# Three taps of a depthwise convolution moved from VectorE to TensorE, and small first-stage operations to ScalarE

## The chip, the core and the metric

The kernel runs on one core of a Trainium2 chip. The metric is device microseconds of one execution on that core. TensorE, VectorE, ScalarE and GpSimd are called by their names or, as the profile has them, PE, DVE, ACT and POOL; SP (SyncE) issues nearly all DMAs. PEld is TensorE's weight load, which overlaps its products.

## What is computed

A trunk of one layer on 1024 frames of width 1024, all float32: a combined input projection feeds a convolution group and an RWKV-7 group side by side, then follow a joint output projection, cross-attention into 256 memory tokens and a squared-ReLU MLP. The part that the change touches is the convolution group's depthwise convolution, and next to it the token shift of the RWKV group:

```python
def conv_group(pa, conv_w, conv_b, ln_g, ln_b):
    u = pa[..., :CONV_WIDTH] * jax.nn.sigmoid(pa[..., CONV_WIDTH:])
    u = lax.conv_general_dilated(          # 31 taps, causal, 512 channels
        u, conv_w[:, None, :].astype(u.dtype), window_strides=(1,),
        padding=[(CONV_K - 1, 0)], dimension_numbers=('NWC', 'WIO', 'NWC'),
        feature_group_count=CONV_WIDTH) + conv_b
    ...                                    # layer norm over channels, silu

def rwkv7_group(pb, mu_b, ...):
    prev = jnp.pad(pb, ((0, 0), (1, 0), (0, 0)))[:, :-1]
    z = (pb + mu_b * (prev - pb)).astype(jnp.float32)
    ...                                    # r, k, v, three LoRA gates, the recurrence
```

## The kernel before

Channels lie on the 128 partitions and frames along the free axis. The 512 convolution channels are four blocks `c`; the frames are two halves `h` of 512.

**First stage (`mixer_in`, line 521).** Eight row blocks of `x` are normalised and transposed into `hT`. For each `c` and `h`, `conv` (line 540) runs two projections of 24 products each (`project`, three fp32r products for each of eight 128-row pieces): the gate, to which ScalarE applies a sigmoid into a tile `sg`, and the value, which VectorE multiplies into `sg` (line 545). A DMA writes `sg` to the DRAM array `du`. Between the (c, h) steps stand five products of the LoRA gates (`lora_out`, line 660). The tiles `sg`, the LoRA results and the later `z` share one ring of four buffers (`ZB`). Then come the r, k, v projections of the first half (`pair_steps(..., 0)`, twelve projections) and, in the second half, twelve more beside the start of the recurrence. Each of them ends in `shift_mix` (line 505): ScalarE scales the projection into `z`, VectorE adds the shifted part (line 511), then ScalarE copies the last column into `prev` (line 515, first half) or VectorE corrects column 0 from it (line 517, second half). The weights of the next projections pass `weight` (line 259): ScalarE rounds `wst` to `whi` (line 266), GpSimd subtracts for `wlo` (line 267), and TensorE needs both.

**The taps (`tap_steps`, line 609).** VectorE runs the convolution in five blocks: two of 512 frames for c = 0 and three of 1024 for c = 1 to 3. Of each block it loads `u` from `du`, makes the first tap with the bias (line 624), adds 30 taps one by one into `acc` (line 627), and a DMA stores `acc` to the DRAM array `dc` (line 632). There is one buffer of `u` and one of `acc`. `conv_norms` reads `dc` later.

**What sets the order.** A scheduler orders each engine's instructions ahead of time by priority; an engine then runs its list strictly in that order. `tap` (line 605) hands out the next taps at a priority 1000 steps ahead of the work around them, so that they fill VectorE early. PSUM banks are handed out in a fixed ring of eight while this stage lasts (`bank`, line 65). Other lines touched: `mixer_constants` (line 166, four scaled masks on VectorE) and `memory_in` (line 433, two scalings of 1024 columns on VectorE).

**After it.** The recurrence (`front`, `chain`) runs over eight blocks of 128 frames, with side work between its steps, until about 600 us; then output projection, attention and the MLP.

Of the kernel before, what the change touches and what calls it, by code (L numbers as in the profile page):

```python
# [9 lines left out]
F32 = mybir.dt.float32  # L10
# [17 lines left out]
GROUPS = PAIRS // GROUP  # L28
ORDER = ((1, 5, 6, 7, 4, 2, 3), (1, 6, 7, 5, 4, 2, 3))
TAPS = 31  # L30
HEADS = 8
N = 64
C = 64
# [18 lines left out]
class Trunk:  # L52
# [100 lines left out]
    def mixer_constants(self, pb, tmp):  # L153
        nc, a = self.nc, self.a

        bones = tmp.tile([P, P], F32, name="bones")
        nc.vector.memset(bones, 0.0)
        nc.vector.memset(bones[0:64, 0:64], 1.0)
        nc.vector.memset(bones[64:128, 64:128], 1.0)
        self.cent = pb.tile([P, P], F32, name="cent")  # L160
        nc.vector.scalar_tensor_tensor(self.cent, bones, -1.0 / N, self.ident, ALU.mult, ALU.add)
        self.bones_r = pb.tile([P, 4, P], F32, name="bones_r")
        self.bones_k = pb.tile([P, 4, HEADS], F32, name="bones_k")
        nc.vector.memset(self.bones_k, 0.0)
        for p in range(4):
            nc.vector.tensor_scalar(self.bones_r[:, p, :], bones, self.col("r_k", p), None, ALU.mult)
            kk = self.col("k_k", p)
            nc.vector.tensor_scalar(
                self.bones_k[:, p, 2 * p : 2 * p + 2], bones[:, 0:128:64], kk, kk, ALU.mult, ALU.mult
            )  # L170

        self.spread = pb.tile([HEADS, 4, P], F32, name="spread")
        nc.sync.dma_start(
            self.spread, a["k_k"][0:1, :].rearrange("o (p f) -> o p f", f=P).broadcast_to([HEADS, 4, P])
        )

        nc.gpsimd.affine_select(
            self.spread, self.spread, pattern=[[P, 4], [1, P]], compare_op=ALU.is_ge, fill=0.0,
            base=0, channel_multiplier=-N,
        )  # L180
        nc.gpsimd.affine_select(
            self.spread, self.spread, pattern=[[-P, 4], [-1, P]], compare_op=ALU.is_ge, fill=0.0,
            base=N - 1, channel_multiplier=N,
        )

        self.mask = pb.tile([P, P], F32, name="mask")
        nc.gpsimd.memset(self.mask, 1.0)
        for lo in (0, 64):
            m = self.mask[lo : lo + 64]
            nc.gpsimd.affine_select(  # L190
                m[:, 0:64], m[:, 0:64], pattern=[[1, 64]], compare_op=ALU.is_gt, fill=0.0,
                base=0, channel_multiplier=-1,
            )
            nc.gpsimd.affine_select(
                m[:, 64:128], m[:, 64:128], pattern=[[1, 64]], compare_op=ALU.is_ge, fill=0.0,
                base=0, channel_multiplier=-1,
            )

        self.reset = pb.tile([P, 8, C], F32, name="reset")
        nc.gpsimd.memset(self.reset, 1.0)  # L200
        nc.gpsimd.memset(self.reset[:, :, 0:1], 0.0)
# [223 lines left out]
    def memory_in(self, px):  # L425
# [3 lines left out]
        for i in range(2):  # L429
            t = px.tile([P, D], F32, tag="x", name="mem", bufs=4)  # L430
            nc.sync.dma_start(t, self.a["mem"][0, i * P : (i + 1) * P, :])
            _, r = self.rms_scale(px, t)
            nc.vector.tensor_scalar(t, t, r, None, ALU.mult)
            ts.append(t)
        for k in range(KC):
            pp = self.bank(self.ps, "mm")
# [68 lines left out]
    def shift_mix(self, dst, pp, j, h, m):  # L505
# [8 lines left out]
        if h == 0:  # L514
            nc.scalar.copy(self.prev[:m, j : j + 1], pp[:, HALF - 1 : HALF])
        else:
            nc.vector.scalar_tensor_tensor(
                dst[:, 0:1], self.prev[:m, j : j + 1], mu, dst[:, 0:1], ALU.mult, ALU.add
            )

    def mixer_in(self, pc, pb, px, pl, pW, pz, hT):
        nc, a = self.nc, self.a
# [17 lines left out]
        def conv(c, h, wg, wv):  # L540
# [3 lines left out]
            pv = self.project(wv, hT, h, P)  # L544
            nc.vector.tensor_tensor(sg, pv, sg, ALU.mult)
            nc.sync.dma_start(self.du[c, :, h * HALF : (h + 1) * HALF], sg)
            self.conved.add((c, h))

        def conv_weights(c):
# [8 lines left out]
                t = norm(i + 1)  # L558
        self.constants(pc, px)
        ts = [norm(4), norm(5)]  # L560
        conv(0, 0, *w)
        self.tap(TE[0], TE[3])
        self.mixer_constants(pb, px)
        features(ts.pop(0), 4)
# [8 lines left out]
        features(ts.pop(0), 6)  # L573
        features(ts.pop(0), 7)
        zl[0] += (self.lora_gate(pl, lora, hT, 0),)
        conv(0, 1, *w)
        zl.append(self.lora_in(pl, lora, hT, 1) + (self.lora_gate(pl, lora, hT, 1),))
        lora = itertools.chain.from_iterable(self.lora_out(pz, h, *zl[h]) for h in range(2))
        for c in range(1, 4):
            w = conv_weights(c)  # L580
            for h in range(2 if c < NC else 1):
                conv(c, h, *w)
                for _ in range(LO):
                    next(lora, None)
                self.tap(2 * TAPA)
            if c == 3:
                self.memory_in(px)
        self.conv, self.conv_weights = conv, conv_weights
        for _ in self.pair_steps(pW, pz, hT, 0):
            next(lora, None)  # L590
            self.tap(TAPA)
# [3 lines left out]
    def second_half(self, pW, pz, hT):  # L595
        pairs = self.pair_steps(pW, pz, hT, 1)
        for c in range(NC, 4):
            self.conv(c, 1, *self.conv_weights(c))
            yield
            for _ in range(12 // (4 - NC)):  # L600
                next(pairs)
# [7 lines left out]
    def tap_steps(self, pV):  # L609

        nc = self.nc
        for c in range(4):
            for h in range(2) if c < HC else (None,):
# [7 lines left out]
                else:  # L621
                    nc.sync.dma_start(u, self.du[c, :, t0 - TAPS + 1 : t0 + n])
                acc = pV.tile([P, S], F32, tag="acc", name="acc")[:, 0:n]
                nc.vector.tensor_scalar(acc, u[:, 0:n], self.cw[:, c : c + 1], self.col("conv_b", c), ALU.mult, ALU.add)
                yield
                for t in range(1, TAPS):
                    nc.vector.scalar_tensor_tensor(  # L627
                        acc, u[:, t : t + n], self.cw[:, t * 4 + c : t * 4 + c + 1], acc, ALU.mult, ALU.add
                    )
                    if t < TAPS - 1:  # L630
                        yield
                nc.sync.dma_start(self.dc[c, :, t0 : t0 + n], acc)
                yield
# [940 lines left out]
```

## Time and profile before

| | |
|---|---|
| median of 3 runs | 1570.99 us (1570.08 to 1573.53) |
| the profiled execution | 1570.75 us |
| its span, first to last instruction | 1569.0 us |
| mean granted TensorE clock | 0.978 of 2.4 GHz |
| TensorE busy | 1496.6 us, 95% of the span |
| VectorE busy | 1168.3 us, 74% |
| ScalarE busy | 665.6 us, 42% |
| GpSimd busy | 533.1 us, 34% |

The shares are averages over stages that differ. A stage is read by a window: busy time of each engine in a stretch, and the clock that TensorE was granted in it (1.00 is 2.4 GHz, 0.50 is 1.2 GHz). What an engine lacks to the length of the stretch is idle time. A timeline row that ends in brackets gives the idle time just before it and what ended it; its first number is the start and the second the length of the row, for all its instructions together (their ends overlap, since an engine is pipelined).

### The profile page before, as it was taken

What the parts mean: (1) busy time and instruction counts of PE and PEld (TensorE: products, weight loads), DVE (VectorE), ACT (ScalarE), POOL (GpSimd) and SP (SyncE); (2) the same over time, 40 slices, a digit from 0 to 9 for tenths busy, and PEclk for the clock granted to TensorE, in tenths of its full rate; (3) what the DMA queues carried; (4) which work ended last, traced back from release to release, by engine and by line L of the source; (5) the groups of instructions that cost most, each with busy time, mean ns of one, the idle gap of its engine ahead of it and who ended that gap; (6) DMA issues with size and microseconds to landing.
All of it is one profiled execution on the core that took longest, in us unless ns stands there. A gap on an engine that the chain in (4) does not pass through costs nothing. (4 is left out here: it accounts for less than half of the span.)

```text
span 1569.0 us, 22055 instructions
## 1 busy us (share of the span) xinstructions
PE 1496.6 (95%) x8114; PEld 1220.9 (78%) x8114; DVE 1168.3 (74%) x1721; ACT 665.6 (42%) x1223; POOL 533.1 (34%) x435
## 2 busy tenths in 40 slices
PE   5998888899999999999999979999999899999998
PEld 4677666778877778888888858888888788888886
DVE  5989898997889988475443787766566487587995
ACT  4423223122556553344230355555555445444454
POOL 4212237432444532431110064545444330003362
PEclk9999998897999999999999989999999999999999
DMA  7144336346334532312110132444444495562323
GB/s 236 47 134 162 115 114 175 113 124 183 108 100 129 151 108 88 101 47 81 41 41 28 48 126 96 163 153 160 148 158 158 155 377 190 185 194 87 102 80 122
DMA packets 175725, 201.14 MB, mean 128 GB/s; under 512 B 12191, under 2 KB 116951, under 8 KB 175618
## 3 DMA queue, kind: packets, MB, share of 16 engines
q1 hardware_dynamic: 168706, 187.15, 38.1%
q10 hardware_dynamic: 6912, 12.59, 2.2%
q8 instruction: 64, 1.05, 0.3%
q14 instruction: 43, 0.35, 0.1%
HBM read 139.92 MB, written 59.77 MB: 127 GB/s over the span
## 5 line engine op out<-in xcount | busy, mean ns | idle before, releaser
L627 DVE SCALAR_TENSOR_TENSOR acc<-u,cw,acc 128x1024 f32<-128x1024 f32 (+1 forms) x150 | 205.0, 1367 | 3.8
L267 POOL TENSOR_TENSOR wlo<-wst,whi 128x1024 fp32r<-128x1024 f32 (+2 forms) x34 | 86.9, 2557 | 133.0 <-ACT whi L266 133.0
L1236 POOL TENSOR_TENSOR p<-p,p 128x512 f32<-128x512 f32 x32 | 60.9, 1932 | 197.8 <-DVE p L1495 174.1
L73 DVE TENSOR_TENSOR s<-f,s 128x512 fp32r<-128x512 f32 x48 | 51.1, 1068 | 53.3 <-ACT s L72 53.3
L1341 ACT ACTIVATE y<-y 128x512 f32<-128x512 f32 x64 | 40.4, 632 | 81.0 <-DVE y L1236 73.3
L73 DVE TENSOR_TENSOR s<-y,s 128x512 fp32r<-128x512 f32 x57 | 44.9, 790 | 22.8 <-ACT s L72 22.8
L95 POOL TENSOR_TENSOR rsr<-rsv,mhalf 128x1 f32<-128x1 f32 x26 | 15.2, 585 | 137.1 <-DVE rsv L90 133.5
L455 PE MATMUL mm<-memT,wkv 128*128 128x256 f32 x256 | 61.7, 387 | 0.0
L1236 POOL TENSOR_TENSOR s<-y 128x512 f32<-128x512 f32 x32 | 41.1, 1306 | 59.8 <-ACT y L1342 56.5
L72 ACT CAST s<-y 128x512 fp32r<-128x512 f32 x57 | 35.2, 621 | 58.2 <-PE us L83 26.8
L266 ACT CAST whi<-wst 128x1024 fp32r<-128x1024 f32 (+2 forms) x34 | 35.0, 1030 | 57.6 <-PE pr L82 12.3
L891 DVE TENSOR_TENSOR fs<-xt,PL 128x4 f32<-128x4 f32 (+15 forms) x128 | 54.8, 428 | 5.8 <-ACT PL L883 3.0
L72 ACT CAST r<-y 128x512 fp32r<-128x512 f32 x55 | 33.8, 620 | 55.7 <-PE cp L83 23.2
L81 PE MATMUL mm<-hT1hi,whi 128*128 128x512 f32 (+1 forms) x120 | 51.1, 426 | 5.2 <-DVE z L511 3.0
L73 DVE TENSOR_TENSOR r<-y,r 128x512 fp32r<-128x512 f32 x55 | 42.8, 782 | 13.7 <-ACT r L72 13.7
L83 PE MATMUL mm<-hT1hi,wlo 128*128 128x512 f32 (+1 forms) x120 | 49.9, 416 | 2.6 <-POOL wlo L267 2.6
L72 ACT CAST s<-w 128x512 fp32r<-128x512 f32 x69 | 42.6, 619 | 21.8 <-DMA w<-in_w_ff_dram 6.9
L455 PEld LDWEIGHTS mm<-memT,wkv 128*128 128x128 f32 x256 | 46.7, 191 | 6.2
L1079 POOL TENSOR_TENSOR wql<-wst,wqh 128x1024 fp32r<-128x1024 f32 x8 | 20.0, 2498 | 88.3 <-ACT wqh L1078 88.3
L82 PE MATMUL mm<-hT1lo,whi 128*128 128x512 f32 (+1 forms) x120 | 49.7, 414 | 0.0
L72 ACT CAST s<-f 128x512 fp32r<-128x512 f32 x64 | 38.0, 620 | 27.4 <-DVE f L1236 21.9
L892 DVE TENSOR_REDUCE xt<-fs 128x2 f32<-128x4 f32 (+15 forms) x128 | 45.2, 353 | 3.1
(1142 smaller groups left out, 4961.7 us busy)
## 6 DMA issues: line engine op xcount, KB each, us to landing
y<-da SPq DMA_DIRECT2D x112, 256.0 KB
wst<-in_w_in_dram SPq DMA_DIRECT2D x32, 512.0 KB
w<-in_w_ff_dram SPq DMA_DIRECT2D x56, 256.0 KB
da<-y ACTq DMA_DIRECT2D x48, 256.0 KB
ms<-in_w_ff_dram SPq DMA_DIRECT2D x16, 512.0 KB
w<-in_w_ff_dram SPq DMA_DIRECT2D x16, 512.0 KB
da<-s SPq DMA_DIRECT2D x32, 256.0 KB
da<-y SPq DMA_DIRECT2D x32, 256.0 KB
```

The lines of the kernel that those rows point to most:

```text
L72: nc.scalar.copy(hi, src)
L73: (eng or nc.vector).tensor_tensor(lo, src, f32(hi), ALU.subtract)
L81: nc.tensor.matmul(ps, lh, rh, start=first and k == 0, stop=False)
L82: nc.tensor.matmul(ps, lh, rl, start=False, stop=False)
L83: nc.tensor.matmul(ps, ll, rh, start=False, stop=last and k == n - 1)
L267: nc.gpsimd.tensor_tensor(lo, st, f32(hi), ALU.subtract)
L455: nc.tensor.matmul(dst, w[:, k, :], mem[k // 4][:, k % 4, :], start=k == 0, stop=k == KC - 1)
L627: nc.vector.scalar_tensor_tensor(acc, u[:, t : t + n], self.cw[:, t * 4 + c : t * 4 + c + 1], acc, ALU.mult, ALU.add)
L891: nc.vector.tensor_tensor(tmp, x, rows, ALU.mult)
L892: nc.vector.tensor_reduce(xt[:, 0:m, 2 * k : 2 * k + 2], tmp, AX.X, ALU.add)
L1236: (eng or self.nc.vector).tensor_tensor(out, x, y, op)
L1341: nc.scalar.activation(c, c, AF.Relu)
```

## The change

With `PETAPS = 3`, the last three taps (offsets 0, 1 and 2 back from the current frame) no longer run on VectorE. A new function `late_taps` builds for each `c` three diagonal 128x128 matrices of the tap weights on ScalarE, multiplies them on TensorE with `sg` shifted by 0, 1 and 2 columns into one PSUM bank (float32 operands), and adds for the second half two narrow products with the last two columns of the first half (`edge`). ScalarE adds the bias into a tile `part` from the ring of four, and a DMA writes it to `dc`. `tap_steps` then loads `acc` from `dc` instead of making the first tap, and adds 28 taps. A block counts as ready (`conved`) after `late_taps`. Besides, the four scaled masks, the two memory scalings and the correction of column 0 in `shift_mix` go from VectorE to ScalarE.

```diff
-            nc.vector.tensor_scalar(self.bones_r[:, p, :], bones, self.col("r_k", p), None, ALU.mult)
+            nc.scalar.activation(self.bones_r[:, p, :], bones, AF.Identity, scale=self.col("r_k", p))
...
-            nc.vector.tensor_scalar(t, t, r, None, ALU.mult)
+            nc.scalar.activation(t, t, AF.Identity, scale=r)
...
         else:
-            nc.vector.scalar_tensor_tensor(
-                dst[:, 0:1], self.prev[:m, j : j + 1], mu, dst[:, 0:1], ALU.mult, ALU.add
-            )
+            nc.scalar.activation(dst[:, 0:1], self.prev[:m, j : j + 1], AF.Identity, bias=dst[:, 0:1], scale=mu)
...
+        def late_taps(c, h, sg):
+
+            if h == 0:
+                self.edge = pl.tile([P, PETAPS - 1], F32, tag="edge", name="edge")
+                nc.scalar.copy(self.edge, sg[:, HALF - PETAPS + 1 :])
+                self.diag = []
+                for j in range(PETAPS):
+                    t = pl.tile([P, P], F32, tag=f"dg{j}", name="diag")
+                    k = (TAPS - 1 - j) * 4 + c
+                    nc.scalar.activation(t, self.ident, AF.Identity, scale=self.cw[:, k : k + 1])
+                    self.diag.append(t)
+            pp = self.bank(self.ps, "mm")
+            for j in range(PETAPS):
+                nc.tensor.matmul(
+                    pp[:, j:], self.diag[j], sg[:, : HALF - j], start=j == 0, stop=h == 0 and j == PETAPS - 1
+                )
+            for j in range(1, PETAPS) if h else ():
+                nc.tensor.matmul(
+                    pp[:, :j], self.diag[j], self.edge[:, PETAPS - 1 - j :], start=False, stop=j == PETAPS - 1
+                )
+            z = pz.tile([P, HALF], F32, tag="z", name="part", bufs=ZB)
+            nc.scalar.activation(z, pp, AF.Identity, bias=self.col("conv_b", c))
+            nc.sync.dma_start(self.dc[c, :, h * HALF : (h + 1) * HALF], z)
             self.conved.add((c, h))
...
-                conv(c, h, *w)
-                for _ in range(LO):
+                made = conv(c, h, *w)
+                for k in range(LO):
+                    if k == 2:
+                        late_taps(*made)
                     next(lora, None)
...
-                nc.vector.tensor_scalar(acc, u[:, 0:n], self.cw[:, c : c + 1], self.col("conv_b", c), ALU.mult, ALU.add)
-                yield
-                for t in range(1, TAPS):
+                nc.sync.dma_start(acc, self.dc[c, :, t0 : t0 + n])
+                for t in range(TAPS - PETAPS):
                     nc.vector.scalar_tensor_tensor(
                         acc, u[:, t : t + n], self.cw[:, t * 4 + c : t * 4 + c + 1], acc, ALU.mult, ALU.add
                     )
```

The scheduler orders the new program anew; from the attention on, the lists of all engines read as before.

On TensorE, before the change, the products of step (1, 1) follow the five LoRA products after step (1, 0) without a break (`hT1` is the second half of the frames, `zw` and `za` feed the LoRA products):

```order
L666 MATMUL cp<-zw,l_w_decay 128x512
L666 MATMUL mm<-zw,l_w_decay 128x512
L666 MATMUL pr<-zw,l_w_decay 128x512
L666 MATMUL py<-zw,l_w_decay 128x512
L666 MATMUL us<-za,l_a_lora 128x512
L81 MATMUL mm<-hT1hi,whi 128x512
```

With the change the three products with the diagonals of step (1, 0) stand eighteen products into the gate projection of step (1, 1), and the first of them waits for VectorE, which makes `sg`:

```order
L83 MATMUL cp<-hT1lo,whi 128x512
L84 MATMUL cp<-hT1hi,wlo 128x512
L561 MATMUL us<-sg,diag 128x512 [waits DVE_49]
L561 MATMUL us<-sg,diag 128x511
L561 MATMUL us<-sg,diag 128x510
L82 MATMUL cp<-hT1hi,whi 128x512
```

All products behind it in TensorE's list wait with it; there are eight such places.

On VectorE, where the last convolution step (3, 1) ends and the first r, k, v projections follow, before the change (`acc<-u,cw,acc` is a tap, `sg` the product of value and gate, `z` the shift of a projection):

```order
L627 SCALAR_TENSOR_TENSOR acc<-u,cw,acc 128x1024 x8
L545 TENSOR_TENSOR sg<-mm,sg 128x512
L627 SCALAR_TENSOR_TENSOR acc<-u,cw,acc 128x1024 x5
L511 SCALAR_TENSOR_TENSOR z<-pr,pcol,z 128x511
L624 TENSOR_SCALAR acc<-u,cw,pcol 128x1024
L627 SCALAR_TENSOR_TENSOR acc<-u,cw,acc 128x1024
L511 SCALAR_TENSOR_TENSOR z<-py,pcol,z 128x511
```

With the change:

```order
L652 SCALAR_TENSOR_TENSOR acc<-u,cw,acc 128x1024 x6
L544 TENSOR_TENSOR sg<-cp,sg 128x512
L652 SCALAR_TENSOR_TENSOR acc<-u,cw,acc 128x1024 x8
L512 SCALAR_TENSOR_TENSOR z<-pr,pcol,z 128x511
L652 SCALAR_TENSOR_TENSOR acc<-u,cw,acc 128x1024 x4
L512 SCALAR_TENSOR_TENSOR z<-py,pcol,z 128x511
```

Before, the block c = 1 ends with the five taps ahead of the first `z`; now it ends with the six ahead of `sg`, and the next block's first eight taps, with the wait for its loads, stand ahead of the first `z`.

On VectorE, in the first block of the recurrence, beside the r, k, v projections of the second half, before the change (`kk`, `AR`, `a`, `BK`, `kp`, `T` belong to the recurrence):

```order
L813 TENSOR_TENSOR kk<-pr,zk 128x512
L627 SCALAR_TENSOR_TENSOR acc<-u,cw,acc 128x1024
L511 SCALAR_TENSOR_TENSOR z<-mm,pcol,z 128x511
L517 SCALAR_TENSOR_TENSOR z<-prev,pcol,z 128x1
L834 SCALAR_TENSOR_TENSOR AR<-kk,W 128x8x64
L835 TENSOR_TENSOR a<-a,kk 128x512
L627 SCALAR_TENSOR_TENSOR acc<-u,cw,acc 128x1024
L836 TENSOR_TENSOR BK<-a,sig 128x8x64
L627 SCALAR_TENSOR_TENSOR acc<-u,cw,acc 128x1024
L511 SCALAR_TENSOR_TENSOR z<-mm,pcol,z 128x511
```

With the change:

```order
L838 TENSOR_TENSOR kk<-pr,zk 128x512
L512 SCALAR_TENSOR_TENSOR z<-mm,pcol,z 128x511
L652 SCALAR_TENSOR_TENSOR acc<-u,cw,acc 128x1024
L859 SCALAR_TENSOR_TENSOR AR<-kk,W 128x8x64
L860 TENSOR_TENSOR a<-a,kk 128x512
L861 TENSOR_TENSOR BK<-a,sig 128x8x64
L512 SCALAR_TENSOR_TENSOR z<-mm,pcol,z 128x511
L847 SCALAR_TENSOR_TENSOR sig<-reset,sig 128x512
L845 TENSOR_TENSOR kp<-kp,zk 128x512
L874 TENSOR_TENSOR T<-pr,mask 128x512 x2
```

The tap ahead of `AR` is now the last of all. Behind the `z` of the twelfth projection 28 taps were left before, and 14 are left now.

## Rows read from the trace of the kernel before

**Rows 1.** Windows by stage: busy us (instructions) of PE, PEld, DVE, ACT, POOL; clock; DMA.

```profile
50.00:165.00 115.00, 103.61 (x444) 79.98 (x442) 104.32 (x107) 37.57 (x64) 23.99 (x11) 0.98 0.36 115
165.00:250.00 85.00, 75.07 (x309) 59.02 (x308) 72.67 (x49) 21.21 (x36) 31.81 (x20) 0.96 0.47 139
250.00:350.00 100.00, 87.31 (x395) 67.86 (x397) 96.88 (x117) 28.30 (x45) 51.19 (x30) 0.91 0.41 121
350.00:400.00 50.00, 50.00 (x422) 43.40 (x421) 38.83 (x76) 15.15 (x31) 17.86 (x23) 0.81 0.60 162
400.00:600.00 200.00, 198.89 (x1828) 159.19 (x1827) 180.13 (x359) 114.24 (x226) 88.62 (x100) 1.00 0.40 123
600.00:900.00 300.00, 299.82 (x1700) 252.23 (x1699) 166.21 (x303) 95.57 (x203) 47.55 (x37) 1.00 0.18 56
```

**Rows 2.** Groups of DVE, 40 to 350 us: busy us, mean ns; idle before, releaser.

```profile
L627 DVE SCALAR_TENSOR_TENSOR acc<-u,cw,acc 128x1024 f32<-128x1024 f32 x90 | 152.5, 1694 | 2.1
L517 DVE SCALAR_TENSOR_TENSOR z<-prev,pcol,z 128x1 f32<-128x1 f32 x12 | 4.1, 342 | 0.0
L624 DVE TENSOR_SCALAR acc<-u,cw,pcol 128x1024 f32<-128x1024 f32 x3 | 3.9, 1303 | 10.0 <-DMA u<-du 10.0
```

**Rows 3.** Timeline of PE and DVE, 130 to 163 us: two waits for `sg`.

```profile
134.21 1.13 PE L666 MATMUL us<-zg,gl 96*128 96x512 f32 x2 [2.40 <-DVE sg L545]
162.91 0.69 PE L438 MATMUL mm<-ident,mem 128*128 128x128 f32 x2 [7.55 <-DVE sg L545]
...
133.47 0.68 DVE L545 TENSOR_TENSOR sg<-us,sg 128x512 f32<-128x512 f32 x1
150.39 10.55 DVE L627 SCALAR_TENSOR_TENSOR acc<-u,cw,acc 128x1024 f32<-128x1024 f32 x5
162.17 0.68 DVE L545 TENSOR_TENSOR sg<-mm,sg 128x512 f32<-128x512 f32 x1
```

**Rows 4.** Waits, 40 to 350 us (ACT) and 165 to 350 us (PE): us, times, longest.

```profile
ACT prev L515 <- DVE z L511: 48.5, 12, 6.3
ACT sg L671 <- DMA du<-sg: 19.0, 3, 9.2
...
PE mm L83 <- POOL wlo L267: 6.0, 4, 2.3
```

**Rows 5.** Timeline of PE: products of 512 columns in fp32r and float32; narrow ones.

```profile
86.10 0.40 PE L666 MATMUL mm<-zw,l_w_decay 98*128 98x512 f32 x1
86.34 0.39 PE L666 MATMUL pr<-zw,l_w_decay 98*128 98x512 f32 x1
98.63 1.02 PE L666 MATMUL pr<-zg,gl 96*128 96x512 f32 x2
99.49 1.02 PE L666 MATMUL py<-zg,gl 96*128 96x512 f32 x2
487.83 0.80 PE L966 MATMUL us<-UV,BT 128*64 128x64 f32 x14
```

**Rows 6.** Timeline of DVE and SP where one block of taps follows another.

```profile
85.67 0.55 DVE L624 TENSOR_SCALAR acc<-u,cw,pcol 128x512 f32<-128x512 f32 x1 [3.94 <-DMA dc<-acc]
119.46 0.81 DVE L624 TENSOR_SCALAR acc<-u,cw,pcol 128x1024 f32<-128x1024 f32 x1 [4.07 <-DMA u<-du]
...
82.11 0.43 SPq L632 DMA_DIRECT2D dc<-acc  x1
115.20 0.42 SPq L620 DMA_DIRECT2D u<-du  x1
```

**Rows 7.** Timeline of DVE and POOL: taps alone, one beside `wlo`, the last.

```profile
135.38 9.21 DVE L627 SCALAR_TENSOR_TENSOR acc<-u,cw,acc 128x1024 f32<-128x1024 f32 x7
183.57 3.30 DVE L627 SCALAR_TENSOR_TENSOR acc<-u,cw,acc 128x1024 f32<-128x1024 f32 x1
326.04 1.28 DVE L627 SCALAR_TENSOR_TENSOR acc<-u,cw,acc 128x1024 f32<-128x1024 f32 x1
...
182.86 2.93 POOL L267 TENSOR_TENSOR wlo<-wst,whi 128x1024 fp32r<-128x1024 f32 x1 [3.05 <-ACT whi L266]
```

**Rows 8.** Windows of 5 us around the end of the stage, columns as in rows 1.

```profile
345.00:350.00 5.00, 2.41 (x16) 2.21 (x17) 5.00 (x10) 2.04 (x4) 0.63 (x2) 0.85 0.63 178
355.00:360.00 5.00, 5.00 (x50) 4.71 (x50) 3.36 (x4) 1.72 (x4) 1.74 (x4) 0.50 1.19 294
```

**Rows 9.** Groups of ACT, 40 to 520 us: the prices of what ScalarE takes over.

```profile
L710 ACT ACTIVATE x<-mm,pcol 128x128 f32<-128x128 f32 x20 | 7.5, 458 | 0.3 <-PE mm L708 0.3
L671 ACT ACTIVATE sg<-mm 128x512 f32<-128x512 f32 x5 | 3.0, 597 | 5.9 <-DMA du<-sg 5.8
```

**Rows 10.** Timeline of PE and DVE at the start: a wait behind the masks.

```profile
25.79 0.50 PE L82 MATMUL pr<-hT0lo,whi 128*128 128x512 f32 x1 [1.77 <-DVE hT0lo L73]
...
23.36 0.74 DVE L166 TENSOR_SCALAR bones_r<-bones,pcol 128x128 f32<-128x128 f32 x1
24.22 0.72 DVE L166 TENSOR_SCALAR bones_r<-bones,pcol 128x128 f32<-128x128 f32 x1
```

More of the change, by code (lines that the diff above doesn't have):

```diff
@@ L30 @@
 TAPS = 31
+PETAPS = 3
 HEADS = 8
@@ L546, in conv @@
             nc.sync.dma_start(self.du[c, :, h * HALF : (h + 1) * HALF], sg)
+            return c, h, sg
+        def late_taps(c, h, sg):
[20 more added lines that the diff above has]
+            nc.sync.dma_start(self.dc[c, :, h * HALF : (h + 1) * HALF], z)
             self.conved.add((c, h))
@@ L560, in mixer_in @@
         ts = [norm(4), norm(5)]
-        conv(0, 0, *w)
+        late_taps(*conv(0, 0, *w))
         self.tap(TE[0], TE[3])
@@ L575, in mixer_in @@
         zl[0] += (self.lora_gate(pl, lora, hT, 0),)
-        conv(0, 1, *w)
+        late_taps(*conv(0, 1, *w))
         zl.append(self.lora_in(pl, lora, hT, 1) + (self.lora_gate(pl, lora, hT, 1),))
@@ L587, in mixer_in @@
                 self.memory_in(px)
-        self.conv, self.conv_weights = conv, conv_weights
+        self.conv, self.conv_weights, self.late_taps = conv, conv_weights, late_taps
         for _ in self.pair_steps(pW, pz, hT, 0):
@@ L597, in second_half @@
         for c in range(NC, 4):
-            self.conv(c, 1, *self.conv_weights(c))
+            self.late_taps(*self.conv(c, 1, *self.conv_weights(c)))
             yield
@@ L629, in tap_steps @@
                     )
-                    if t < TAPS - 1:
+                    if t < TAPS - PETAPS - 1:
                         yield
```

## The prediction

> **What bounds the kernel now.** I read the windows by stage first [rows 1]. From 400 to 600 us TensorE is idle 1.1 us of 200, from 600 to 900 us 0.2 of 300: there it alone sets the pace, and a product added to it costs its whole length. From 50 to 400 us it is not full. A stage's loss is its idle time (length less busy time) plus what a low clock cost ((1 - clock) times busy time):
>
> A, 50 to 165 us (convolution steps): 11.4 + 2.1 = 13.5. B, 165 to 250 (r, k, v of the first half): 9.9 + 3.0 = 12.9. C, 250 to 350 (second half beside the recurrence's start): 12.7 + 7.9 = 20.6. D, 350 to 400: 0 + 9.5. In all 56.5 us, the most that any relief of other engines can bring.
>
> VectorE is busy 104 of 115, 73 of 85 and 97 of 100 us in A to C, and taps are most of it [rows 2]. The waits name it: at 134.21 and 162.91 us TensorE stands 2.40 and 7.55 us for an `sg` that comes late, behind taps [rows 3]. In B the way is longer: ScalarE waits 48.5 us in all for VectorE's `z` ahead of `prev`, and behind `prev` in its list stands `whi`, behind that GpSimd's `wlo`, for which TensorE waits 6.0 us [rows 4]. So the change gives the engine that ends the program more work, to relieve the one that holds it up in its first 400 us.
>
> **What TensorE gets.** Eight convolution steps with three products of up to 512 float32 columns. In fp32r such a product follows the one before after 0.24 us (86.10 to 86.34); in float32, as here, after 0.86 (98.63 to 99.49) [rows 5]. 24 x 0.86 = 20.6. The four `edge` pairs are 8 products of one or two columns, two records each, like the row with 0.80 us for 14 records [rows 5]: 16 x 0.057 = 0.9. Together **+21.6 us**, all by 165 us.
>
> **Stage A.** The two waits on `sg` (10.0 us) came of a freed PSUM bank; a step now uses eight banks of the ring of eight instead of seven, so which work meets which bank changes, and I let them and the clock's 2.1 go: -12. New is a direct wait: the diagonal products stand 15 to 24 products behind the end of the value projection (counted in TensorE's new order), some 5.3 to 6.4 us by 0.24 us each and 0.86 for the float32 LoRA products among them [rows 5]. `sg` is late by 3 to 10 us behind its projection where taps stand ahead of it, as the 10.55 us of five taps just ahead of the one at 162.17 show [rows 3]. All of TensorE's list waits behind that product. I take 4 us over the eight places (none if `sg` always comes within its 5 us; 10 if it stays as late as now). **A: -8** (-12 to -2).
>
> **The joins of the tap blocks.** There is one `acc`. Before, a join cost 3.94 us (the store issued at 82.11 lands at 85.67, 3.6 us for 256 KB) or 4.07 us (the load of `u` issued at 115.20 lands at 119.46, 4.3 us for 512 KB) [rows 6]; the three first taps of 1024 waited 10.0 us together [rows 2]. Now the store must land and then `acc` must be loaded, one transfer after the other. Added idle time of VectorE: 3.6 at the first join, about 6 at the second (its load also waits for `part` of step (1, 1): products, ScalarE, a write), 4.3 at each of the other two: 18 us, all within A and B. The loads wait in SP's queue in order, so the loads of `sg` for the gates, `dz` and weights behind them wait too; ScalarE already waits 19.0 us for such a load [rows 4]. I price each load by the slower of the two transfers shown. The Trainium skill, "DMA: Bandwidth & Descriptors", section "Anatomy of one DMA — SWDGE (gpsimd) path", gives 2.0 us plus bytes at 436 GB/s (for another issuer than SP): an estimate of 3.2 us for 512 KB. The row's 4.26 is longer; by the page each large join would idle 1.1 us less, and my sum would come out some 2 us lower.
>
> **Stage B.** VectorE does 8 taps and waits for the third block's loads ahead of the first `z`, where five taps stood, and then 3 to 4 taps per `z` as before. Three or four taps and a `z` take 5 to 7 us (7 taps 9.21 us, alone [rows 7]), against 24 x 0.24 = 5.8 us of TensorE per projection. Five more large taps than before fall ahead of the twelfth `z`. B loses most of its former 12.9 again, and the joins' 8.6 us partly add to it: **B: +5** (0, if its 12 us of VectorE idle time take the joins in, to +12).
>
> **Stage C.** 14 taps remain behind the twelfth `z` instead of 28. What is a removed tap worth? Seven in a row take 9.21 us, 1.3 each; beside a `wlo` of GpSimd (182.86, 2.93 long) one takes 3.30 [rows 7]; the mean is 1694 ns [rows 2]. I take 1.3, since GpSimd's `wlo` remain and will stretch another tap: 14 x 1.3 = 18.2, plus 4.1 for L517 [rows 2], about 22 us. The Trainium skill, "SBUF — State Buffer", section "Who interferes with whom", says that a VectorE instruction with two SBUF inputs contends with a GpSimd instruction that reads SBUF, the later one being blocked. The stretched row agrees; by the mean, 14 taps would be 23.7 us, and TensorE could be given its whole 20.6, which makes the sum 5 us lower.
>
> TensorE can take at most 20.6. Against it speaks that ScalarE now corrects column 0 and so waits for VectorE's `z` in the second half too; behind it in its list stand `whi`, the next scaling and the recurrence's exponentials. In B waits of this kind cost TensorE 6.0 us on `wlo` [rows 4]. I leave 4.6 of the loss: **C: -16** (-8 to -20.6).
>
> **Stage D** is low clock alone: 2.41 us busy of 345 to 350, then 0.50 (1.2 GHz) at 355 to 360 [rows 8]. With the gap gone most of it goes: **D: -7** (0 to -9.5).
>
> **ScalarE.** 8 `part` at 597 ns, 12 diagonals, four masks and at most 12 columns at 458 ns or less [rows 9], four `edge` likewise, two scalings of 1024 at about twice 597: at most 22 us, beside 87 of 300 busy [rows 1]. Hidden; without that cover, the `part` on a join's path would cost 0.6 each. The masks leave VectorE's start, where two of them take 0.7 us each and TensorE waits 1.77 us for what stands behind [rows 10]: **-1** (0 to -2). The ring of four now takes seven tiles a step, and `part` holds one until its write has landed, some 3.6 us: no separate price, since it acts through ScalarE's slack.
>
> **Sum.** On the profiled execution's 1570.75 us (the median is 1570.99, 0.2 more, left aside): 1570.75 + 21.6 - 8 + 5 - 16 - 7 - 1 = 1565.4, **1565 us**. With all bounds at their good end +21.6 - 12 - 20.6 - 9.5 - 2 = -22.5 (1548); near their bad ends +21.6 - 2 + 12 - 8 = +23.6 (1594).
>
> **Rivals.** *Slower: the round trips eat the relief.* Off VectorE go 9 large taps' worth (11.7), 6 half ones (3.9), 4.1 of columns, 3.5 of scalings and masks: 23 us, and the joins take 18 back. If they hold up the `z` and `sg` behind them, since VectorE's list is strict, taps end where they ended before, C gives back some 5 and D nothing: 1570.75 + 21.6 - 8 + 5 - 5 - 1 = 1583. For it: VectorE's order puts eight taps and a join ahead of the first `z`. Against: VectorE had 23 us idle in A and B [rows 1], into which waits can fall. It decides from joins of over 8 us each, or a last tap later than now (326 us [rows 7]). Chance 0.31.
>
> *No change: the recurrence's own start binds C.* Its first block needs `zk`, which by the order comes by way of the eleventh `z` and a DMA; if that chain, not the taps, made C's gaps, C gives 12 and D 5: 1570.75 + 21.6 - 8 + 5 - 12 - 5 - 1 = 1571. For it: the last interval before the clock fell, 345 to 350 us [rows 8], comes 19 us after the last tap began. Chance 0.15.
>
> *Much faster.* Joins fall into idle time, and A to D keep little loss: 1548. Against: VectorE stays over 85% busy there. Chance 0.08.
>
> **How the numbers follow.** The forecast has 0.46, of which 0.06 ends within 0.2% (3 us, about what a measurement of this kernel can tell from no change). Faster 0.40 + 0.08 = 0.48; same 0.06 + 0.15 = 0.21; slower 0.31. The range runs from 1547, leaving out half of the fastest case, to 1586, leaving out a third of the slow case (its joins longer, or `sg` as late as now): about 0.15 outside.
>
> **What would show it.** TensorE's busy time up by 21 to 22 us, and 0.86 per diagonal product; if 0.24, the first step is wrong. Waits of TensorE for `sg` at the diagonals (L561) of 4 us together; over 10, A is wrong. First taps of a block (L652) waiting 7 to 9 us for the load of `acc`; over 8 each with late `z` behind them is the slow rival. The last tap well ahead of 326 us plus what A and B grow; a stage C with under 5 us lost; a clock of 1.00 after it. If the clock after C still falls to 0.50, D's 7 us stay lost.

## The result and the profile after

The changed kernel takes 1591.0 us (median of 4 runs, 1587.5 to 1593.0) against 1572.0: a ratio of 1.0121, 95% interval 1.0107 to 1.0135. It is 19 us slower; 1565 was predicted, with a range of 1547 to 1586. The profiled execution took 1592.15 us, its span is 1590.4, TensorE's mean clock 0.982. TensorE is busy 1518.1 us, 21.5 more than before, VectorE 1145.4, 22.9 less: what the edits should do to each engine they did. Both came out as expected, and the time did not.

The same stretches as in [rows 1], now of the changed kernel:

```profile
50.00:165.00 115.00, 112.69 (x453) 81.48 (x452) 95.50 (x100) 43.13 (x79) 18.15 (x9) 0.99 0.37 122
165.00:250.00 85.00, 75.65 (x318) 58.07 (x317) 67.58 (x48) 23.54 (x42) 27.64 (x13) 0.98 0.47 142
250.00:350.00 100.00, 87.49 (x384) 68.54 (x382) 89.38 (x94) 34.11 (x58) 57.91 (x38) 0.90 0.47 136
350.00:400.00 50.00, 47.95 (x419) 39.35 (x418) 36.13 (x72) 17.13 (x34) 15.19 (x22) 0.97 0.60 164
400.00:600.00 200.00, 195.12 (x1692) 155.08 (x1691) 170.67 (x340) 107.30 (x212) 80.07 (x94) 0.99 0.41 126
600.00:900.00 300.00, 296.91 (x1806) 249.55 (x1806) 168.23 (x315) 99.53 (x215) 57.58 (x45) 0.99 0.18 54
```

From 50 to 165 us TensorE's idle time fell from 11.4 to 2.3 us. The low clock of 350 to 400 us is gone (0.97 instead of 0.81), as stage D wanted. But 250 to 350 us loses as much as before (12.5 idle, clock 0.90), and from 400 to 600 us TensorE now misses 4.9 us and some clock, where it missed 1.1.

Since the work has moved by some 20 us, windows between equal places of the program say more. They run from the start to the last `sg`, from there to VectorE's part of the twelfth `z` of the r, k, v projections, and from there to the second `qh` of the attention; behind that both take 847 to 848 us. First the kernel before, then the changed one:

```profile
0.00:162.20 162.20, 135.57 (x592) 103.78 (x592) 134.23 (x165) 64.82 (x109) 43.70 (x43) 1.00 0.45 140
162.20:252.60 90.40, 78.20 (x322) 61.45 (x322) 77.83 (x55) 21.91 (x37) 32.37 (x21) 0.95 0.47 140
252.60:720.60 468.00, 455.76 (x3410) 368.80 (x3411) 391.89 (x674) 202.99 (x387) 190.25 (x183) 0.96 0.39 116
```

```profile
0.00:175.60 175.60, 156.90 (x635) 114.07 (x636) 127.87 (x152) 73.39 (x133) 39.29 (x43) 0.99 0.46 146
175.60:272.40 96.80, 80.60 (x343) 62.36 (x342) 84.29 (x57) 25.84 (x46) 34.73 (x20) 0.97 0.49 143
272.40:743.10 470.70, 455.02 (x3415) 365.78 (x3414) 368.22 (x648) 207.36 (x399) 186.74 (x183) 0.97 0.38 115
```

The convolution stage is 13.4 us longer, B is 6.4 longer (the last of the eight groups of products, at 176.47, falls behind the first mark and so into B), and the third stretch, called the recurrence stretch below, is 2.7 longer although VectorE has 24 us less to do in it. There the forecast had 23 us of gain.

The prices, from the timelines of TensorE, VectorE and SP of the changed kernel (start, length, idle time before and what ended it):

```profile
44.90 2.74 PE L561 MATMUL cp<-sg,diag 128*128 128x512 f32 x6
114.62 4.48 PE L561 MATMUL us<-sg,diag 128*128 128x512 f32 x6 [1.89 <-DVE sg L544]
148.94 2.84 PE L561 MATMUL us<-sg,diag 128*128 128x512 f32 x6 [0.41 <-DVE sg L544]
176.47 2.75 PE L561 MATMUL mm<-sg,diag 128*128 128x512 f32 x6
...
90.61 5.48 DVE L652 SCALAR_TENSOR_TENSOR acc<-u,cw,acc 128x512 f32<-128x512 f32 x7 [5.93 <-DMA acc<-dc]
127.97 1.28 DVE L652 SCALAR_TENSOR_TENSOR acc<-u,cw,acc 128x1024 f32<-128x1024 f32 x1 [10.38 <-DMA acc<-dc]
179.31 5.25 DVE L652 SCALAR_TENSOR_TENSOR acc<-u,cw,acc 128x1024 f32<-128x1024 f32 x4 [2.98 <-DMA acc<-dc]
241.97 7.25 DVE L652 SCALAR_TENSOR_TENSOR acc<-u,cw,acc 128x1024 f32<-128x1024 f32 x4 [6.37 <-DMA acc<-dc]
306.19 1.27 DVE L652 SCALAR_TENSOR_TENSOR acc<-u,cw,acc 128x1024 f32<-128x1024 f32 x1
...
117.61 0.32 SPq L657 DMA_DIRECT2D dc<-acc  x1
120.31 0.32 SPq L570 DMA_DIRECT2D dc<-part  x1
123.89 0.32 SPq L650 DMA_DIRECT2D acc<-dc  x1
```

Three diagonal products take 2.7 us, as forecast. Only two of the eight places wait for `sg`, 2.3 us together. The joins cost VectorE 25.7 us instead of some 14; the second is the long one, since its load is issued only at 123.89, 6.3 us after the store (the write of `part` that it also needs went out at 120.31), and lands 4.1 us later. And the last tap starts at 306 us instead of 326, though the twelfth `z` comes some 20 us later. The relief of VectorE has happened, and over the recurrence stretch as a whole TensorE has nothing of it.

### The profile page after: what moved, and what is told of

The parts are those of the page before. It is cut to its first block, busy times and chain, and to the rows that moved or that the text cites. A ratio compares the mean times of both kernels' runs of the same rounds, so it can differ in the third digit from the quotient of the medians.

```text
span 1590.4 us, 22220 instructions
## 1 busy us (share of the span) xinstructions
PE 1518.1 (95%) x8178; PEld 1228.3 (77%) x8178; DVE 1145.4 (72%) x1686; ACT 682.4 (43%) x1267; POOL 527.5 (33%) x435
## 5 line engine op out<-in xcount | busy, mean ns | idle before, releaser
L652 DVE SCALAR_TENSOR_TENSOR acc<-u,cw,acc 128x1024 f32<-128x1024 f32 (+1 forms) x140 | 192.2, 1373 | 29.8 <-DMA acc<-dc 26.0
L916 DVE TENSOR_TENSOR fs<-xt,PL 128x4 f32<-128x4 f32 (+15 forms) x128 | 58.2, 454 | 8.1 <-ACT PL L908 5.4
L74 DVE TENSOR_TENSOR r<-y,r 128x512 fp32r<-128x512 f32 x55 | 43.2, 789 | 13.4 <-ACT r L73 13.4
L84 PE MATMUL mm<-hT1hi,wlo 128*128 128x512 f32 x112 | 47.5, 424 | 3.1 <-POOL wlo L268 2.3
L82 PE MATMUL mm<-hT1hi,whi 128*128 128x512 f32 x112 | 48.4, 432 | 1.7 <-DVE z L512 1.7
L83 PE MATMUL mm<-hT1lo,whi 128*128 128x512 f32 x112 | 46.9, 418 | 0.0
```

Of the source, the lines that this page charges most:

```text
L74: (eng or nc.vector).tensor_tensor(lo, src, f32(hi), ALU.subtract)
L82: nc.tensor.matmul(ps, lh, rh, start=first and k == 0, stop=False)
L83: nc.tensor.matmul(ps, lh, rl, start=False, stop=False)
L84: nc.tensor.matmul(ps, ll, rh, start=False, stop=last and k == n - 1)
L652: nc.vector.scalar_tensor_tensor(acc, u[:, t : t + n], self.cw[:, t * 4 + c : t * 4 + c + 1], acc, ALU.mult, ALU.add)
L916: nc.vector.tensor_tensor(tmp, x, rows, ALU.mult)
```

## The experiments

Two theories stood at first. **T**: the relief comes off the end of the tap stream and helps TensorE in the convolution stage alone. **J**: it is worth its 23 us, and the round trips of `acc` take it back. All medians stand against 1572 to 1573 us for the kernel before, timed on the same chip each time; in brackets stands the ratio to it, for some with its 95% interval.

**Relief without its price.** The fixes alone (e5), and the fixes with three taps left out on VectorE and nothing put in their place (e1):

```diff
-                for t in range(1, TAPS):
+                for t in range(1, TAPS - 3):
...
```

> The kernel before with the small ScalarE fixes and with VectorE running 28 of the 31 taps of every block; nothing is added to TensorE, no acc is loaded (the three last taps are left out of the result). It measures what VectorE's relief is worth by itself. Theory T (the relief comes off the end of the tap stream, where TensorE was nearly covered already, and helps only in the convolution stage): 8 to 12 us faster than before, about 1562. Theory J (the relief is worth its 23 us, and the round trips of acc at the joins take it back in the changed kernel): 20 to 28 us faster, 1544 to 1552.

> The kernel before with the ScalarE fixes alone (masks, memory scalings, column 0), all 31 taps on VectorE. They take 9 us of work from VectorE. Theory T (relief of VectorE reaches TensorE only in the convolution stage): 0 to 3 us faster than before, about 1571; then the three taps were worth about 5 of the 7.2 us of the run with relief alone. Theory F (the fixes, not the taps, made those 7.2 us): 6 to 8 us faster, about 1566.

Measured: e1 took 1565.9 us (ratio 0.9954, interval 0.9939 to 0.9968), 7 faster, short of both forecasts; e5 took 1583.1 (1.0075, 1.0051 to 1.0099), 11 *slower*, which no theory had. This speaks against J: without any join or product the relief brings 7 us over the kernel before. But T is not the whole either: over the same fixes, three taps fewer bring 17 us. e1 by stage:

```profile
0.00:158.60 158.60, 138.27 (x587) 105.65 (x588) 128.62 (x153) 66.20 (x110) 38.06 (x42) 0.99 0.45 140
158.60:255.40 96.80, 78.37 (x327) 59.87 (x326) 82.98 (x57) 24.29 (x45) 34.48 (x21) 0.96 0.47 136
255.40:716.90 461.50, 449.94 (x3415) 362.25 (x3414) 369.13 (x649) 208.63 (x401) 188.49 (x183) 0.98 0.39 117
```

Even here the recurrence stretch gains 6.5 us, not 23.

**The joins.** e3 makes `acc` with the first tap again instead of loading it (the late taps are lost); e4 keeps the result and halves all blocks, with two buffers each of `u` and `acc`:

```diff
-                nc.sync.dma_start(acc, self.dc[c, :, t0 : t0 + n])
-                for t in range(TAPS - PETAPS):
+                nc.vector.tensor_scalar(acc, u[:, 0:n], self.cw[:, c : c + 1], self.col("conv_b", c), ALU.mult, ALU.add)
+                for t in range(1, TAPS - PETAPS):
```

```diff
-TAPA, TAPB = 5, 4
+TAPA, TAPB = 10, 8
...
-HC, TE = 1, (10, 10, 10, 0)
+HC, TE = 4, (10, 10, 10, 0)
...
-                u = pV.tile([P, TAPS - 1 + S], F32, tag="u", name="u")[:, 0 : TAPS - 1 + n]
+                u = pV.tile([P, TAPS - 1 + HALF], F32, tag="u", name="u", bufs=2)[:, 0 : TAPS - 1 + n]
...
-                acc = pV.tile([P, S], F32, tag="acc", name="acc")[:, 0:n]
+                acc = pV.tile([P, HALF], F32, tag="acc", name="acc", bufs=2)[:, 0:n]
```

> The changed kernel, but acc is not loaded from dc: the first of the 28 taps makes acc with the bias as before the change, and part is written to dc and overwritten (the three late taps are left out of the result). TensorE's products, their waits, part and its write stay; only the second transfer at the joins goes. Theory J (the round trips eat the relief): 12 to 20 us faster than the changed kernel, 1571 to 1579. Theory T: VectorE's shorter joins only move the end of the tap stream, 0 to 5 us faster, 1586 to 1591.

> The changed kernel with all tap blocks of 512 frames and two buffers each of u and acc, so that the loads of a block can land while the block before it is still worked on; the result is complete. Each tap of 512 costs VectorE about 0.88 us instead of half of 1.69, 6 us more in all. Theory J: the idle time at the joins (26 us in the changed kernel) goes, 12 us or more faster than the changed kernel, 1579 or less. Theory T: within 5 us of the changed kernel, 1586 to 1594.

e3 took 1588.2 us (1.0092, 1.0063 to 1.0120), e4 1590.6 (1.0112, 1.0071 to 1.0153): 3 us less than the changed kernel, and the same. e3 is the weaker case, since its joins still wait 19.8 us in all, mostly for `u`. In e4 only 6.7 of the 25.7 us are left, against 5 us of added work, and neither gains J's 12 us. In both the taps end with the twelfth `z`, some 30 us earlier than in the changed kernel:

```profile
117.01 0.81 DVE L650 TENSOR_SCALAR acc<-u,cw,pcol 128x1024 f32<-128x1024 f32 x1 [8.30 <-DMA u<-du]
276.71 1.33 DVE L652 SCALAR_TENSOR_TENSOR acc<-u,cw,acc 128x1024 f32<-128x1024 f32 x1
...
85.43 8.63 DVE L652 SCALAR_TENSOR_TENSOR acc<-u,cw,acc 128x512 f32<-128x512 f32 x11 [2.20 <-DMA acc<-dc]
269.15 4.29 DVE L652 SCALAR_TENSOR_TENSOR acc<-u,cw,acc 128x512 f32<-128x512 f32 x3
```

The round trips are not the cause. From e1 to e3, where products, `part` and its write come in and nothing else, the time grows by 22.3 us: all that was added to TensorE. In the profiled executions, of which e3's is its fastest, the two differ by 16 us in all and by 19.5 up to the twelfth `z` (255.4 and 274.9 us), where the products stand.

**The price of the products.** The forecasts name two further theories from here on. **T2**: TensorE's products and VectorE's relief both count in full, each at the worth that the runs above give it. **R**: every edit makes a new order of the first 600 us, and that by itself is worth up to 10 us either way. e2 keeps one diagonal of three; e11 rounds the diagonals and `sg` to fp32r (`sr` is the rounded copy, with `n` = 2 columns of the first half in front):

```diff
-            for j in range(PETAPS):
-                nc.tensor.matmul(pp[:, j:], self.diag[j], sg[:, : HALF - j], ...)
...
+            nc.tensor.matmul(pp, self.diag[0], sg, start=True, stop=True)
```

```diff
-                    t = pl.tile([P, P], F32, tag=f"dg{j}", name="diag")
+                    t = pl.tile([P, P], F32R, tag=f"dg{j}", name="diag")
...
+            nc.scalar.copy(sr[:, n:], sg)
+                nc.tensor.matmul(pp, self.diag[j], sr[:, n - j : n - j + HALF], start=j == 0, stop=j == n)
```

> The changed kernel with one diagonal product instead of three for each step and without the edge products (two of the three late taps are left out of the result); part, its write, the load of acc and the 28 taps stay. TensorE does 16 products of 0.86 and the edges less, about 14.7 us. Theory T (TensorE's added products stand on the path at full length): 14 to 16 us faster than the changed kernel, about 1576. Theory J (VectorE with its joins sets the pace, TensorE's products lie in its shadow): at most 7 us faster, 1584 or more.

> The changed kernel with the diagonals and a copy of sg rounded to fp32r, so that a product should take 0.24 us instead of 0.86 (24 x 0.62 = 15 us less on TensorE); the copy carries the last two columns of the first half in front, so the eight narrow products go too (1 us). The rounding leaves out the low half of the three taps. ScalarE gets eight copies of 0.6 us, which stand ahead of the products. Theory T2: 15 us faster than the changed kernel, 1572 to 1579. Theory R: off that by more than 5 us. If the products are hidden: 1588 or more.

e2 took 1581.2 us (1.0045), 10 us faster than the changed kernel, two thirds of what it saves TensorE and between the forecasts of T and J. e11 took 1594.1 (1.0143, 1.0099 to 1.0187), not faster at all, 15 us over T2's range. Its products are cheap (TensorE's timeline, and its first and third stretch):

```profile
46.06 0.86 PE L568 MATMUL cp<-sgr,diag 128*128 128x512 f32 x3
...
0.00:171.80 171.80, 145.34 (x609) 110.60 (x609) 129.45 (x153) 80.15 (x148) 38.65 (x46) 0.98 0.47 149
261.90:739.10 477.20, 455.49 (x3421) 368.07 (x3420) 385.43 (x656) 206.68 (x400) 188.90 (x183) 0.97 0.37 113
```

By the twelfth `z` its profiled execution is 10.5 us ahead of the changed kernel (261.9 against 272.4); its recurrence stretch then takes 477 us instead of 471 and gives more than half of that back. (This execution, at 1587.7 us, is the fastest of the four; where the others lose more is not known.) So the products are not hidden, and in this execution what decides comes behind them, as only R would have it.

**More and fewer taps.** e9 adds all 31 taps on VectorE on top of `part` (three count twice); e10 has `PETAPS = 2`:

> The changed kernel, but VectorE adds all 31 taps again on top of part (three taps count twice in the result): TensorE's products, part and the loads of acc stay, VectorE's relief by the taps goes. Theory T2 (with products and loads held equal the taps' relief is worth what it is worth without them, 17 us between the fixes alone at 1583 and relief alone at 1566): 1604 to 1612. Theory J (joins and products leave VectorE's relief without worth): 1589 to 1595.

> The changed kernel with PETAPS = 2: two late taps on TensorE, 29 on VectorE. Theory T2: a tap costs TensorE 7.2 us and relieves by 17.2/3 = 5.7, and the load of acc stays, so about 1.5 us faster than three, 1587 to 1591. Theory R (each edit makes a new order of the whole first 600 us, which by itself is worth up to 10 us either way): off that by more than 5 us.

e9 took 1601.3 us (1.0172), 10 us over the changed kernel and between the two forecasts: the relief has worth, 10 us here. e10 took 1593.9 (1.0136), 3 over the changed kernel instead of 2 under. It misses T2's range by 3 us, less than the 5 that R asked for, and so decides nothing.

**A wait less.** In both kernels ScalarE's copy into `prev` follows VectorE's `z` and waits for it, with the next `whi` behind. Put ahead of `z`, it no longer waits for it (the correction of column 0 in the second half moves likewise):

```diff
         nc.scalar.activation(dst, pp, AF.Identity, scale=self.omm[:m, j : j + 1])
+        if h == 0:
+            nc.scalar.copy(self.prev[:m, j : j + 1], pp[:, HALF - 1 : HALF])
...
         nc.vector.scalar_tensor_tensor(dst[:, 1:HALF], pp[:, 0 : HALF - 1], mu, dst[:, 1:HALF], ALU.mult, ALU.add)
-        if h == 0:
-            nc.scalar.copy(self.prev[:m, j : j + 1], pp[:, HALF - 1 : HALF])
```

> The kernel before with one edit: in the shift of a projection ScalarE copies the last column (or VectorE corrects column 0) ahead of VectorE's z in the program, so that ScalarE's copy no longer waits for z, and the rounding of the next weights behind it does not either. Theory P (in the r, k, v stage VectorE's taps reach TensorE only by ScalarE's wait for z ahead of prev; TensorE needs 5.5 us per projection and takes 7.3): the stage from the first to the twelfth z falls from 80 to 62 to 70 us, and the time by 8 to 16, about 1560. Theory Q (VectorE's z paces it anyway, by the ring of four z tiles): 0 to 3 us, about 1571.

> The changed kernel with the same edit (ScalarE's copy and its correction of column 0 stand ahead of VectorE's z). Theory P: 8 to 16 us faster than the changed kernel, about 1578; the difference to the kernel before with the same edit stays near the 22 us of TensorE's added products or grows, since the relief then has less to relieve. Theory Q: within 3 us of the changed kernel, about 1589.

> The kernel before with the ScalarE fixes and the same edit for prev, no taps on TensorE. Theory P: as the kernel before with the edit alone, or 0 to 3 us faster, 1556 to 1561, faster than both kernels. Theory Q: about 1570.

> As the run before, with ScalarE's prev ahead of VectorE's z as in the run that put prev first in the changed kernel (1585). Theory T2: 15 us below that, 1567 to 1573. Theory R: off that by more than 5 us.

e6 took 1591.3 us (1.0125, 1.0107 to 1.0143), 19 us *slower* than before, with the same instructions and a wait less; e7 took 1584.8 (1.0087), 6 us faster than the changed kernel. e8 at 1585.3 (1.0087) is 15 us over Q's forecast and 24 over P's; e12 at 1587.0 (1.0096) is 14 over T2's range, which leaves R. P falls: the stage from the first to the twelfth `z` keeps its pace in e6 (79.9 us, 80.1 before) and nearly in e7 (78.0, 80.6 in the changed kernel). The detour over `prev` does not set it. Q has the pace right and the times wrong. VectorE with its three to four taps per `z`, busy 78 of 90 us in B, is the likely pacemaker, though no run tests that by itself. But e6 made a second question out of the first: how can so small an edit cost 19 us? The instructions are the same; their order is what is left.

**The order alone.** One number of the priorities ranks the side work beside the recurrence. With another number every instruction stays and 800 to 1300 of TensorE's 6900 products stand elsewhere, from the recurrence's first block on:

```diff
-O = (0, 0, 0, 100, -200)
+O = (0, 0, 0, 100, -300)
```

(e13 in the kernel before, e15 in the changed one; e14 and e16 have -100.)

> The kernel before with one number of the priorities changed: side work beside the recurrence is ranked 300 steps ahead instead of 200. Every instruction stays the same; only the order moves (on TensorE some 830 of 6860 products stand elsewhere, from the first block of the recurrence on). Theory R (the order of the kernel before is an unusually good one; other orders of the same work lose 10 to 20 us beside the recurrence, as with prev first, 1591, and with the fixes alone, 1583): 1580 to 1592. Theory S (orders of the same work differ by 5 us or less, and the losses of those two runs belong to their edits): 1567 to 1577.

> As the run before, with side work ranked 100 steps ahead instead of 200 (some 1310 products moved). Theory R: 1580 to 1592. Theory S: 1567 to 1577.

> The changed kernel with side work ranked 300 steps ahead (same instructions, about 1060 products moved). Theory R: anything from 1580 to 1600, mean with the next run and the changed kernel some 5 to 12 us above the mean of the three orders of the kernel before. Theory S: 1586 to 1596, about 19 above the same orders of the kernel before.

> The changed kernel with side work ranked 100 steps ahead (about 1020 products moved). Theory R: 1580 to 1600. Theory S: 1586 to 1596.

| rule of order | kernel before | changed kernel | difference |
|---|---|---|---|
| as it is | 1572 | 1591.0 | +19 |
| side work earlier | 1592.5 (e13) | 1593.6 (e15) | +1 |
| side work later | 1595.1 (e14) | 1604.8 (e16) | +10 |
| `prev` first | 1591.3 (e6) | 1584.8 (e7) | -6.5 |

R holds against S: e13 and e14 have ratios of 1.0134 (1.0119 to 1.0149) and 1.0150 (1.0134 to 1.0165) for the same work, both a little above R's range. e15 lies in both ranges and e16 above both; the mean of the three orders is 10 us higher with the change, within R's 5 to 12. Of six kernels here with 31 taps on VectorE and none on TensorE the kernel before is the fastest by 11 us. Where the orders part is shown by the windows of the recurrence stretch: e6, e13 and e14 of the kernel before, then e7, e15 and e16 of the changed one:

```profile
253.30:740.30 487.00, 463.84 (x3411) 372.11 (x3412) 388.51 (x674) 199.14 (x383) 192.93 (x183) 0.95 0.37 111
...
253.60:742.00 488.40, 463.66 (x3410) 372.55 (x3411) 395.60 (x674) 203.79 (x389) 192.46 (x183) 0.95 0.36 110
...
253.30:746.90 493.60, 461.99 (x3410) 374.15 (x3411) 393.06 (x674) 202.79 (x386) 190.10 (x183) 0.95 0.37 109
...
270.00:732.90 462.90, 452.51 (x3418) 363.67 (x3419) 370.10 (x649) 208.87 (x400) 186.99 (x183) 0.97 0.39 117
...
271.90:743.00 471.10, 452.69 (x3414) 362.85 (x3413) 371.30 (x648) 206.85 (x399) 191.52 (x183) 0.97 0.38 114
...
271.80:755.80 484.00, 457.24 (x3415) 367.42 (x3414) 365.72 (x648) 204.80 (x398) 188.98 (x183) 0.96 0.37 111
```

With 31 taps the stretch takes 487 to 494 us in these orders and 468 in the kernel before; with 28 it takes 463 to 484, and 471 in the changed kernel. Up to the twelfth `z` the orders agree within 3 us. Cut at the start of the recurrence's third block (its third `AR` on VectorE, behind the low clock of stage D), the stretch falls into two parts that behave differently. The two parts of the kernel before, of the changed one and of e13:

```profile
252.60:382.70 130.10, 118.97 (x640) 95.49 (x641) 118.18 (x165) 36.45 (x62) 59.56 (x42) 0.86 0.49 140
382.70:720.60 337.90, 336.79 (x2772) 273.31 (x2771) 273.70 (x512) 166.54 (x325) 130.69 (x141) 1.00 0.35 106
...
272.40:385.60 113.20, 105.75 (x635) 83.58 (x633) 91.41 (x123) 41.11 (x75) 57.23 (x41) 0.91 0.46 134
385.60:743.10 357.50, 349.26 (x2780) 282.20 (x2781) 276.81 (x526) 166.25 (x325) 129.51 (x143) 0.99 0.36 108
...
253.60:390.40 136.80, 123.92 (x669) 99.93 (x670) 123.73 (x171) 37.28 (x64) 59.64 (x42) 0.88 0.49 138
390.40:742.00 351.60, 339.73 (x2743) 272.62 (x2742) 271.86 (x505) 166.51 (x326) 132.82 (x141) 0.98 0.31 100
```

TensorE's loss in the two parts, idle time plus (1 - clock) times busy time as in the prediction, for all eight kernels of the table above, one profiled execution each (the clock has two digits, so the second part is good to some 2 us):

| rule of order | first part, before | first part, changed | second part, before | second part, changed |
|---|---|---|---|---|
| as it is | 27.8 | 17.0 | 1.1 | 11.7 |
| side work earlier | 27.8 | 13.7 | 18.7 | 17.9 |
| side work later | 27.1 | 16.6 | 26.7 | 29.4 |
| `prev` first | 29.9 | 12.1 | 17.9 | 7.4 |
| mean | 28.1 | 14.9 | 16.1 | 16.6 |

In the first part the change takes 11 to 18 us off the loss under every rule of order. In the second the order decides, with the change or without it: the means differ by half a microsecond, and 1.1 us is the outlier. In the same part (third `AR` to second `qh`) no other kernel of this record loses less than 6.7 us.

In the orders that lose, TensorE stands still in many gaps, the longest of 5.5 us in e14, with a low clock behind some of them. The largest single place in e14 is the way into the attention: windows of 20 us, the kernel before and e14, and e14's waits of TensorE there:

```profile
700.00:720.00 20.00, 20.00 (x103) 16.69 (x102) 15.94 (x24) 10.84 (x19) 2.16 (x4) 1.00 0.34 103
```

```profile
720.00:740.00 20.00, 12.66 (x60) 10.26 (x59) 16.31 (x21) 8.48 (x15) 4.90 (x5) 0.83 0.45 145
...
724.42 0.63 PE L254 MATMUL ep<-ident,junk 128*128 128x128 f32 x4 [1.83 <-DVE junk L246]
731.00 1.09 PE L254 MATMUL py<-ident,junk 128*128 128x128 f32 x4 [5.51 <-DVE junk L246]
```

In e14 TensorE waits 7.3 us there for the normalised rows that VectorE makes (`junk`); in the kernel before it has other work until they come.

## Why the prediction was wrong

Its steps, one by one:

- **What TensorE gets, +21.6: right.** It is 21.5 us more busy, 2.7 us per three products. On the path nearly in full: +22.3 from e1 to e3, two thirds from e2 to the changed kernel.
- **Stage A, -8, stage B, +5, and the start, -1: right.** With the products the time up to the twelfth `z` should grow by 21.6 - 8 + 5 - 1 = 17.6 us; it grew by 19.8, and by 16.7 to 18.5 in the other three pairs of equal rules. In A the direct waits cost 2.3 us, not 4. In B the reason given holds: the first `z` comes 16.2 us behind the last `sg` instead of 10.4, behind eight taps and a join, and then the projections keep their pace (80.6 us from the first to the twelfth `z`, 80.1 before). The start's part is too small to tell. Wrong is the way by which VectorE was said to hold up TensorE in B: e6 and e7 show that the detour over `prev` does not set the pace. And the 6.0 us of [rows 4], given there for B, are the waits on one bank (`mm`) in B and C; B alone has 7.0 over all banks.

```profile
172.52 0.75 DVE L511 SCALAR_TENSOR_TENSOR z<-pr,pcol,z 128x511 f32<-128x511 f32 x1 [3.19 <-ACT z L510]
...
175.63 0.69 DVE L544 TENSOR_TENSOR sg<-cp,sg 128x512 f32<-128x512 f32 x1 [5.28 <-PE cp L84]
191.78 0.74 DVE L512 SCALAR_TENSOR_TENSOR z<-pr,pcol,z 128x511 f32<-128x511 f32 x1
```

- **The joins, 18 us of added idle time: too high.** They add 11.8 (the second 6.3, as forecast; the others 1 to 2 each, not 4), and e4, with 6.7 us of them left in all, gains nothing. The 512 KB load took 4.1 us at the second join (123.89 to 127.97), near the 4.3 of [rows 6]. The estimate of 3.2 us from the Trainium skill, "DMA: Bandwidth & Descriptors", section "Anatomy of one DMA — SWDGE (gpsimd) path", is too short for it.
- **Stages C and D, -16 and -7: the step that failed.** The stretch that holds them should shrink by 23 us and grew by 2.7. Two things were wrong. First, C and D were sized too high. The reasons given there did come true: the last tap came 20 us earlier, the low clock of D went, and up to the third block TensorE's loss fell, but from 27.8 to 17.0 us, 10.8 instead of 23 (13 in the mean of the four pairs). Second, a term was put at nothing. I read the 1.1 us of idle time of the kernel before between 400 and 600 us as what the work costs there ("it alone sets the pace") and left that stretch as it was. It belonged to the order: the same instructions in two other orders lose 18.7 and 26.7 us in the second part (e13, e14). The new program was ordered anew, and there it loses 11.7, 10.6 more than before, which takes back what C and D gave.
- **The slow rival** had the sign and a time of 1583, by luck: its mechanism did not come about. One join of four is over 8 us, the last tap comes earlier and not later, and e4 gains nothing by its short joins. That an edit gives up an unusually good order was no case of mine, so the range ended at 1586.

Over the four pairs of the first table the change costs 6 us on average, between -6.5 and +19. By place the same comes out: some 18 more up to the twelfth `z`, 13 less in the first part of the recurrence stretch, and nothing in the second. So some 6 of the 19 us belong to the change, and some 13 to the good order that it gave up. This is an estimate from four orders that differ by up to 25 us. The single runs fit it only roughly: 22 for the products and 3 for the loads, less a relief of 10 (e9) to 17 (e1 against e5), is 8 to 15, and leaves the fixes out, which cost 11 by themselves under the rule as it is (e5) and gain 6 with `prev` first (e6 to e8). Open stays which property makes the order of the kernel before so good. None of the complete versions tried here beats it.

## What to carry to other kernels

Where a scheduler orders the program, the time of a tuned kernel is that of its work and of its order. A small edit redraws the order: run two or three neutral reorderings of the kernel before ahead of trusting any sum, and take their spread into the range, here 23 us against a forecast gain of 6. A stretch without idle time in the profile before is no promise that it stays so in a new order. A relief of an engine is worth what it takes off the waits that end last. Here the taps filled every free slot, and the three taken away came off the end of their list: the last one 20 us earlier, at an unchanged pace of the projections ahead of it.

## What the hardware showed

Two small things. A tap of 512 columns takes VectorE 897 ns in the changed kernel, not half of the 1690 of one of 1024 (groups of VectorE, 40 to 330 us), 6% more per column:

```profile
L652 DVE SCALAR_TENSOR_TENSOR acc<-u,cw,acc 128x1024 f32<-128x1024 f32 x84 | 142.0, 1690 | 21.9 <-DMA acc<-dc 19.7
L652 DVE SCALAR_TENSOR_TENSOR acc<-u,cw,acc 128x512 f32<-128x512 f32 x56 | 50.2, 897 | 7.9 <-DMA acc<-dc 6.2
```

And a wait cost TensorE more than its length: behind the 1.89 us before 114.62 the three diagonal products take 4.48 us instead of 2.74, with a granted clock of 0.63 meanwhile, between its two levels:

```profile
114.60:119.20 4.60, 4.58 (x9) 2.05 (x9) 2.88 (x4) 0.40 (x1) 0.12 (x1) 0.63 0.79 237
```
